# A hybrid decoder trunk on one Trainium2 core: square roots of the mixer's norms by Newton steps instead of ScalarE's Sqrt

## The chip, the core and the metric

The kernel runs on one core of a Trainium2 chip. The core's engines take instructions from queues of their own: TensorE (PE, matrix products; its weight loads are shown apart as PEld), VectorE (DVE), ScalarE (ACT, activation functions and copies), GpSimd (POOL) and SyncE (SP, which issues most DMAs). They wait for one another by semaphores. The metric is the time of one execution on the device in microseconds (us), lower is better. ACT computes functions by tables; where the next function is not in the table that is loaded, an instruction ACT_TABLE_LOAD stands ahead of it, with the line of the function that needs it.

## What is computed

A trunk of two layers on x of 512 tokens by 1024 (one sequence), in float32. Layer 0 mixes tokens by a gated DeltaNet, layer 1 by sliding-window attention on a shared key and value; each layer ends with a convolutional gated MLP. The part that the change touches is the mixer:

```python
q = l2norm(q) * 128 ** -0.5          # l2norm: x * rsqrt(sum(x * x) + 1e-6)
k = l2norm(k)                        # 8 key heads, each serving 2 of 16 value heads
...
o = chunked_gated_delta_rule(q, k, v, g, beta)
...
o = rmsnorm(o, out_norm_w) * silu(z) # rmsnorm: mean over the 128 of a head
return o @ w_out
```

## The kernel before, in words

Every product with a weight matrix is made of three passes: the weights and the moving tile are each split into a rounded part and a rest (whi/wlo and xh/xl, or yh/yl), and whi·xh, whi·xl and wlo·xh are added (L162 to L164). ACT casts the rounded part (L132 for weights, L168 for rows), DVE subtracts for the rest (L133, L169). A pass moves 512 columns. Tokens stand in 4 chunks of 128 (NC = 4).

The mixer treats its heads in four groups g = 0 to 3, each of 2 key heads and 4 value heads. For a group the jobs are: key projections K (convolution and silu at L277 to L281), key norms B, the decay matrices and key products P (exponentials at L475), a triangular solve I (DVE, L555 to L561, levels L at L587 to L615), queries Q, query norms R, A, key tokens T, values V (turned on PE at L198, then scaled by ACT at L538), the scan C0 to C3 over the four chunks, and output norms N; then z (gate projection, silu L705) and g (gate: the output is loaded from DRAM, scaled by ACT at L720, turned on PE at L198, multiplied on DVE at L723).

A table of words (ORDER, five lines) and a table of shifts (SHIFT) give each job a priority. A scheduler makes the order of each engine's instructions from these priorities and from its own reckoning of how long each takes; so an instruction that is added or taken out can move others on all engines.

**Key norms** (key_norms, L426 to L456): PE multiplies the keys with themselves (L433), DVE takes the diagonal and sums it (L437, L443) into sse, adds EPS (L444) and takes the reciprocal rk2 (L445) for brk and kap (L449, L455). ACT takes the square root nk (L446), which only the scaling of the turned values reads (L538): the values are multiplied by the norm of the key.

**Output norms** (out_norms, L685 to L699): sso holds the sums of squares of the outputs (from ACT, L682). f_c becomes the mean plus a term with EPS (L688, L690), then its square root (ACT, L698) and the reciprocal of it (DVE, L699). f_c is read by the gates (ACT, L720) and by six one-column copies on POOL that hold the later loads of x back (L839).

**Scan** (L622 to L683), one step for each chunk: PE multiplies the state with keys and queries (kS, qS, L635), DVE makes rq (L638), ACT qe (L648), PE pu (L651), ACT copies it to us (L653), PE makes the new state pS and the output po from it (L659), DVE adds (L663, L666, L677, L679), ACT squares for the norm (L682), and SP stores the output to od (L683). Between these stand passes of projections.

**The end of the mixer.** The output projection starts with rows of gated outputs: those of groups 0 to 2 come back from DRAM (yd) and are split (L168, L169) into tiles such as kT, qT, nt, sy, at; the four of group 3 are read from od into dt, scaled, turned and gated without a way through DRAM. Later, rstd_cols takes a square root on ACT (L871) for the norm ahead of the MLP.

Of the kernel before, what the change touches and what calls it, by code (L numbers as in the profile page):

```python
# [8 lines left out]
F32 = mybir.dt.float32  # L9
F32R = mybir.dt.float32r  # L10
BF16 = mybir.dt.bfloat16
AF = mybir.ActivationFunctionType
ALU = mybir.AluOpType
AX = mybir.AxisListType
# [3 lines left out]
P = 128  # L18
T = 512
NC = T // P  # L20
# [21 lines left out]
def kernel(  # L42
# [27 lines left out]
    V, S, G, PE, SP = nc.vector, nc.scalar, nc.gpsimd, nc.tensor, nc.sync  # L70
# [9 lines left out]
    def nm(s):  # L80
        cnt[0] += 1
        return f"{s}_{cnt[0]}"
# [24 lines left out]
    def row(tag, dt=F32, n=T):  # L107
        return main.tile([P, n], dt, tag=tag, bufs=ROWS[tag], name=nm(tag))

    def pair(tag, dt=F32):  # L110
        return main.tile([P, 2, T], dt, tag=tag, bufs=PAIRS[tag], name=nm(tag))

    def bank(tag):
        return psum.tile([P, T], F32, tag=tag, bufs=BANKS[tag], name=nm(tag))

    def const(shape, dt=F32, s="c"):
        return cp.tile(list(shape), dt, name=nm(s))
# [53 lines left out]
    def split_scaled(src, col, hi, lo):  # L171
        S.activation(hi[:], src, AF.Identity, scale=col)  # L172
        V.scalar_tensor_tensor(lo[:], src, col, hi[:].bitcast(F32), op0=ALU.mult, op1=ALU.subtract)
# [8 lines left out]
    def together(makes, *after):  # L182
        first = None
        for make in makes:
            if first is None:
                first = make()
                for a in after:
                    behind(first, a)
            else:
                with tc.high_priority(JUMP):  # L190
                    behind(make(), first)
# [31 lines left out]
    warm = const([P, 1], s="warm")  # L223
    S.activation(warm[:], epsc[:], AF.Sqrt)


    def columns(parts, n, s, q=SP, tag="acc", place="g"):
        st = row(tag, n=P)
        r = 0
        for ap in parts:  # L230
            k = ap.shape[0]
            q.dma_start(st[r : r + k, :], ap)
            r += k
        ps = bank(place)
        PE.transpose(ps[:, :n], st[:n, :], ident[:n, :n])
        t = const([P, n], s=s)
        V.tensor_copy(t[:], ps[:, :n])
        return t
# [16 lines left out]
    for c in range(NC):  # L255
        junk = main.tile([P, D], F32, tag="nt", bufs=2, name=nm("junk"))
        r = const([P, 1], s="rx")
        S.activation(junk[:], xs[c], AF.Square, accum_out=r[:])
        S.activation(r[:], r[:], AF.Sqrt, bias=epsc[:, 0:1], scale=1.0 / D)
        V.reciprocal(r[:], r[:])  # L260
# [14 lines left out]
    def conv_silu(ps, t, o):  # L275
        acc = row("acc")
        S.activation(acc[:], ps[:], AF.Identity, scale=cw_c[:, 96 + t : 97 + t])  # L277
        for d in range(1, 4):
            col = cw_c[:, 32 * (3 - d) + t : 32 * (3 - d) + t + 1]
            V.scalar_tensor_tensor(acc[:, d:], ps[:, : T - d], col, acc[:, d:], op0=ALU.mult, op1=ALU.add)  # L280
        S.activation(o, acc[:], AF.Silu)  # L281
        return o
# [114 lines left out]
    tmp6 = row("p6s")  # L397
    sso = const([P, 16, NC], s="sso")
    f_c = const([P, 16, NC], s="fc")
    sse = const([P, 2, 8, NC], s="sse")  # L400
    nk = const([P, 8, NC], s="nk")
    rk2 = const([P, 8, NC], s="rk2")
# [20 lines left out]
    )  # L423
    fcw = [columns([fconv_rows[l, 0:128, :]], 128, "fcw", tag="f") for l in range(2)]

    def key_norms(g):  # L426
        pr = slice(2 * g, 2 * g + 2)
        st[g]["kk"] = pair("m32")
        for i in range(2):
            kT = st[g]["k"][:, i, :]  # L430
            ps = bank("g")
            cut = [slice(c * P, (c + 1) * P) for c in range(NC)]
            together([lambda cs=cs: PE.matmul(ps[:, cs], kT[:, cs], kT[:, cs], start=True, stop=True) for cs in cut])  # L433
            S.copy(st[g]["kk"][:, i, :], ps[:])
            diag = row("va")
            d3 = diag[:].rearrange("p (c t) -> p c t", c=NC)
            V.tensor_tensor(  # L437
                d3,
                ps[:].rearrange("p (c t) -> p c t", c=NC),
                ident[:].unsqueeze(1).to_broadcast([P, NC, P]),  # L440
                op=ALU.mult,
            )
            V.tensor_reduce(sse[:, 0, 2 * g + i, :], d3, axis=AX.X, op=ALU.add)  # L443
        V.tensor_scalar(sse[:, 0, pr, :], sse[:, 0, pr, :], EPS, None, op0=ALU.add)  # L444
        V.reciprocal(rk2[:, pr, :], sse[:, 0, pr, :])  # L445
        S.activation(nk[:, pr, :], sse[:, 0, pr, :], AF.Sqrt)  # L446
        for i in range(2):
            hs = slice(4 * g + 2 * i, 4 * g + 2 * i + 2)
            V.tensor_tensor(  # L449
                brk[:, hs, :],  # L450
                beta_t[:, hs, :],
                rk2[:, 2 * g + i : 2 * g + i + 1, :].to_broadcast([P, 2, NC]),
                op=ALU.mult,
            )
            V.tensor_tensor(kap[:, hs, :], brk[:, hs, :], egd[:, hs, :], op=ALU.mult)  # L455
# [228 lines left out]

    def out_norms(g):  # L685
        hs = slice(4 * g, 4 * g + 4)
        fs = f_c[:, hs, :].rearrange("p (i j) c -> p i j c", i=2)
        V.tensor_scalar(f_c[:, hs, :], sso[:, hs, :], 1.0 / P, None, op0=ALU.mult)  # L688
        for j in range(2):
            V.scalar_tensor_tensor(  # L690
                fs[:, :, j, :],
                sse[:, 1, 2 * g : 2 * g + 2, :],
                P * EPS,
                fs[:, :, j, :],
                op0=ALU.mult,
                op1=ALU.add,
            )
        S.activation(f_c[:, hs, :], f_c[:, hs, :], AF.Sqrt)  # L698
        V.reciprocal(f_c[:, hs, :], f_c[:, hs, :])  # L699


    def gate_proj(h):
# [32 lines left out]
    def bias_rows():  # L735
# [22 lines left out]
        "L": levels,  # L758
        "C": scan,
        "B": key_norms,  # L760
        "R": query_norms,
        "N": out_norms,
    }
    heads = {"z": 0, "g": 0}
# [679 lines left out]
```

## Time and profile before

| quantity | value |
|---|---|
| time, median of 3 runs | 1415.96 us (1414.63, 1415.96, 1419.01) |
| span of the profiled execution | 1412.6 us; the page gives no other time for it |
| HBM read and written | 133.60 MB and 15.75 MB |
| ACT_TABLE_LOADs in the program | 36 |
| busiest groups | three matmul passes L162, L163, L164: 444.2, 444.0 and 441.9 us shown |

Times in a row of the profile are in us from the start of the span unless marked ns. A group of instructions is told as line, engine, operation, output <- inputs, shape, count, then busy time and mean ns, then the idle time of the engine just ahead of it and what ended it (a bracket in the timeline says the same). Matmuls are pipelined and their ends are modelled: a pass of 512 columns is shown 0.39 long, while the next one starts 0.23 later. So for PE the distance of starts tells more than the duration.

### The profile page before, as it was taken

The numbers are of one execution on the slowest core, as the hardware profiler recorded it, in microseconds if no ns is written. First come the engines' busy times: TensorE is split into PE (matmuls) and PEld (weight loads), VectorE is DVE, ScalarE is ACT, GpSimd is POOL, SyncE is SP. The second block draws the span as 40 slices with busy tenths as digits, with TensorE's granted clock in tenths as the row PEclk, the third lists the DMA queues.
The fourth block names the chain that finished last, engine by engine and source line by source line (L and its number), as shares of the span: only waits on it lengthen the run. The fifth ranks groups of instructions, "written<-read, shape, count | busy, mean of one in ns | idle before, by whom it ended". The sixth has DMA issues, their size and how long they took to land.

```text
span 1412.6 us, 21751 instructions
## 1 busy us (share of the span) xinstructions
PE 1384.7 (98%) x8370; PEld 1167.1 (83%) x8370; DVE 1108.1 (78%) x2070; ACT 748.1 (53%) x1470; POOL 15.6 (1%) x37
## 2 busy tenths in 40 slices
PE   7999999999999999999999999999999999999998
PEld 5787888878877888888988889777788888988897
DVE  4996896978856438879878889788668888878996
ACT  7764566656658225444344446567544444444543
POOL 1000000000100000000000000000000000000000
PEclk9999999999999999999999999999999999999999
DMA  5333254172465323221443223322132231432222
GB/s 161 92 103 115 79 175 126 61 231 84 140 225 159 119 90 112 90 90 46 135 150 119 75 79 109 109 71 76 61 112 90 90 101 49 146 106 82 92 75 75
DMA packets 162299, 151.80 MB, mean 107 GB/s; under 512 B 24148, under 2 KB 150677, under 8 KB 162197
## 3 DMA queue, kind: packets, MB, share of 16 engines
q1 hardware_dynamic: 159938, 150.22, 33.2%
q8 instruction: 66, 1.08, 0.3%
q10 hardware_dynamic: 2259, 0.20, 0.1%
q14 instruction: 36, 0.29, 0.1%
HBM read 133.60 MB, written 15.75 MB: 106 GB/s over the span
## 4 chain that ended last, share of the span: by engine, by line
PE 87%; DVE 6%; DMA 2%; ACT 2%; issue 1%; SPq 0%; DVEq 0%; ACTq 0%
PE d L162 20%; PE d L163 20%; PE d L164 20%; PE g L198 2%; DVE wlo L133 2%; PE d L1054 1%; PE d L1207 1%; PE d L1211 1%; PE d L1209 1%; PE d L1052 1%; PE d L1053 1%; PE s L1054 1%; PE s L1052 1%; PE s L1053 1%; PE s L659 1%
## 5 line engine op out<-in xcount | busy, mean ns | idle before, releaser
L162 PE MATMUL d<-xh,whi 128*128 128x512 f32 x1128 | 444.2, 394 | 0.2
L163 PE MATMUL d<-xl,whi 128*128 128x512 f32 x1128 | 444.0, 394 | 0.0
L164 PE MATMUL d<-xh,wlo 128*128 128x512 f32 x1128 | 441.9, 393 | 0.3 <-DVE wlo L156 0.3
L132 ACT CAST whi<-stage 128x1024 fp32r<-128x1024 f32 (+2 forms) x234 | 227.4, 976 | 247.7 <-PE d L163 165.1
L133 DVE TENSOR_TENSOR wlo<-stage,whi 128x1024 fp32r<-128x1024 f32 (+2 forms) x234 | 263.4, 1128 | 70.4 <-ACT whi L132 69.6
L162 PEld LDWEIGHTS d<-xh,whi 128*128 128x128 f32 x1128 | 211.7, 188 | 44.9 <-ACT xh L172 0.5
L164 PEld LDWEIGHTS d<-xh,wlo 128*128 128x128 f32 x1128 | 211.6, 188 | 44.6 <-DVE wlo L156 0.7
L163 PEld LDWEIGHTS d<-xl,whi 128*128 128x128 f32 x1128 | 211.7, 188 | 43.2 <-issue 0.5
L280 DVE SCALAR_TENSOR_TENSOR acc<-d,cwc,acc 128x511 f32<-128x511 f32 (+2 forms) x96 | 70.7, 739 | 8.7 <-ACT acc L277 7.9
L913 DVE TENSOR_TENSOR sz<-d,p6s 128x512 f32<-128x512 f32 x59 | 40.6, 688 | 42.9 <-PE d L164 40.7
L935 ACT ACTIVATE dt<-dt 128x512 f32<-128x512 f32 x44 | 27.8, 631 | 78.3 <-DVE dt L918 78.3
L918 DVE SCALAR_TENSOR_TENSOR dt<-sz,fcw,dt 128x511 f32<-128x511 f32 (+1 forms) x60 | 44.8, 747 | 1.8 <-ACT dt L916 0.9
L918 DVE SCALAR_TENSOR_TENSOR va<-sz,fcw,va 128x511 f32<-128x511 f32 (+1 forms) x58 | 43.3, 747 | 0.9
L561 DVE TENSOR_TENSOR sT<-sT,p6s 64x31 f32<-64x31 f32 (+15 forms) x124 | 40.9, 330 | 2.0
L555 DVE TENSOR_TENSOR p6s<-sN,sT 64x31 f32<-64x31 f32 (+15 forms) x124 | 40.7, 328 | 1.9
L1276 ACT ACTIVATE dt<-dt,sm 128x256 f32<-128x256 f32 (+1 forms) x64 | 30.1, 471 | 21.5 <-DVE sm L1259 21.5
L132 ACT CAST whi<-st 128x768 fp32r<-128x768 f32 (+1 forms) x30 | 23.7, 792 | 30.5 <-PE g L1053 9.0
L913 DVE TENSOR_TENSOR zl<-d,p6s 128x512 f32<-128x512 f32 x29 | 20.0, 688 | 17.8 <-PE d L164 17.8
L682 ACT ACTIVATE rq<-o 128x128 f32<-128x128 f32 x64 | 19.0, 301 | 25.4 <-DVE o L677 22.3
L937 DVE TENSOR_TENSOR va<-dt,va 128x512 f32<-128x512 f32 x44 | 30.4, 690 | 1.2
L133 DVE TENSOR_TENSOR wlo<-st,whi 128x768 fp32r<-128x768 f32 (+1 forms) x30 | 26.8, 899 | 2.2 <-ACT whi L132 2.2
L916 ACT ACTIVATE dt<-sz,normc,fcw 128x512 f32<-128x512 f32 x30 | 24.5, 815 | 6.5 <-DVE sz L913 6.0
(770 smaller groups left out, 2876.2 us busy)
## 6 DMA issues: line engine op xcount, KB each, us to landing
stage<-in_ffn_w_up_dram SPq DMA_DIRECT2D x44, 1024.0 KB, 4.8
stage<-in_a_w_in_dram SPq DMA_DIRECT2D x23, 1024.0 KB, 5.8
stage<-in_ffn_w_down_dram SPq DMA_DIRECT2D x16, 768.0 KB, 4.3
stage<-in_a_w_out_dram SPq DMA_DIRECT2D x8, 1024.0 KB, 5.0
st<-in_ffn_w_down_dram SPq DMA_DIRECT2D x8, 768.0 KB, 5.3
zd<-sz SPq DMA_DIRECT2D x16, 256.0 KB, 2.6
od<-o SPq DMA_DIRECT2D x16, 256.0 KB
stage<-in_b_w_q_dram SPq DMA_DIRECT2D x4, 1024.0 KB, 5.0
```

What stands on the lines that cost most here:

```text
L132: S.copy(hi[:, :kt, :m], src)
L133: V.tensor_tensor(lo[:, :kt, :m], src, hi[:, :kt, :m].bitcast(F32), op=ALU.subtract)
L162: PE.matmul(ps, hi[:, k, :m], xh[k], start=first and k == 0, stop=False)
L163: PE.matmul(ps, hi[:, k, :m], xl[k][:], start=False, stop=False)
L164: done.append(PE.matmul(ps, lo[:, k, :m], xh[k], start=False, stop=last and k == kt - 1))
L280: V.scalar_tensor_tensor(acc[:, d:], ps[:, : T - d], col, acc[:, d:], op0=ALU.mult, op1=ALU.add)
L555: V.tensor_tensor(tv, N[:, s, s + 1 : 32].unsqueeze(2).to_broadcast([64, n, m]), Tm[:, s : s + 1, 0:m].to_broadcast([64, n, m]), op=ALU.mult,)
L561: V.tensor_tensor(Tm[:, s + 1 : 32, 0:m], Tm[:, s + 1 : 32, 0:m], tv, op=ALU.subtract)
L913: V.tensor_tensor(u[:], ps[:], rs[:], op=ALU.mult)
L918: V.scalar_tensor_tensor(acc[:, d:], u[:, : T - d], tap(2 - d, t), acc[:, d:], op0=ALU.mult, op1=ALU.add)
L937: V.tensor_tensor(b[:], a[:], b[:], op=ALU.mult)
L1276: S.activation(ej, ej, AF.Exp, bias=ngm[:, i : i + 1], scale=-1.0, accum_out=den[:, i : i + 1])
```

## The change

A helper gives the inverse square root: a first guess from the bits of the number read as an integer (one tensor_scalar on DVE), then three Newton steps of four small operations on an engine that is given. For key norms these twelve run on GpSimd, in 128x8 tiles, and a thirteenth multiplies by sse to make the square root from its inverse. For output norms they run on VectorE, in 128x16 tiles, and give f_c at once, so that the reciprocal is not needed; the mean is kept in a new tile fx. The square root at rstd_cols stays as it is.

```diff
+I32 = mybir.dt.int32
...
+    fx = const([P, 16, NC], s="fx")
...
+    def inverse_root(y, x, t, E):
+        V.tensor_scalar(y.bitcast(I32), x.bitcast(I32), -0.5, 1597463007.0, op0=ALU.mult, op1=ALU.add)
+        for _ in range(3):
+            E.tensor_tensor(t, y, y, op=ALU.mult)
+            E.tensor_tensor(t, t, x, op=ALU.mult)
+            E.tensor_scalar(t, t, -0.5, 1.5, op0=ALU.mult, op1=ALU.add)
+            E.tensor_tensor(y, y, t, op=ALU.mult)
+
+    root_t = const([P, 16, NC], s="roott")
...
         V.reciprocal(rk2[:, pr, :], sse[:, 0, pr, :])
-        S.activation(nk[:, pr, :], sse[:, 0, pr, :], AF.Sqrt)
+        inverse_root(nk[:, pr, :], sse[:, 0, pr, :], root_t[:, pr, :], G)
+        G.tensor_tensor(nk[:, pr, :], nk[:, pr, :], sse[:, 0, pr, :], op=ALU.mult)
...
-        fs = f_c[:, hs, :].rearrange("p (i j) c -> p i j c", i=2)
-        V.tensor_scalar(f_c[:, hs, :], sso[:, hs, :], 1.0 / P, None, op0=ALU.mult)
+        fs = fx[:, hs, :].rearrange("p (i j) c -> p i j c", i=2)
+        V.tensor_scalar(fx[:, hs, :], sso[:, hs, :], 1.0 / P, None, op0=ALU.mult)
...
-        S.activation(f_c[:, hs, :], f_c[:, hs, :], AF.Sqrt)
-        V.reciprocal(f_c[:, hs, :], f_c[:, hs, :])
+        inverse_root(f_c[:, hs, :], fx[:, hs, :], root_t[:, hs, :], V)
```

In the changed program lines are numbered one higher up to the helper and 12 or 13 higher behind it, so L538 becomes L551 and L659 becomes L672. PE has the same products in both.

**First place: the first group's key norms on ACT.** Before (nk is the square root, dt an exponential of the decay, va the silu of a value projection; the numbers behind a name only tell tiles apart):

```order
L475 ACTIVATE dt_449<-g_446,ngc_331 128x128 x4
L475 ACTIVATE dt_463<-g_460,ngc_331 128x128 x4
L446 ACT_TABLE_LOAD
L446 ACTIVATE nk_351<-sse_350 128x8
L475 ACT_TABLE_LOAD
L475 ACTIVATE dt_478<-g_475,ngc_331 128x128 x4
L475 ACTIVATE dt_492<-g_489,ngc_331 128x128 x4
L281 ACT_TABLE_LOAD
L281 ACTIVATE va_540<-acc_572 128x512
```

With the change:

```order
L488 ACTIVATE dt_464<-g_461,ngc_331 128x128 x4
L488 ACTIVATE dt_478<-g_475,ngc_331 128x128 x4
L488 ACTIVATE dt_493<-g_490,ngc_331 128x128 x4
L488 ACTIVATE dt_507<-g_504,ngc_331 128x128 x4
L282 ACT_TABLE_LOAD
L282 ACTIVATE va_555<-acc_587 128x512
```

The square root and two table loads are gone ahead of va, and the four exponentials stand together.

**Second place: the last group's scan on PE, from step 0 to step 1.** Rows with line L162 to L164 are passes of a projection, s_ and p_ are banks of the scan. Before, from the last pass ahead of pu (L651) to the passes behind po (L659):

```order
L164 MATMUL d_4404<-xh_196,wlo_4406 128x512
L651 MATMUL s_4176<-rq_4166,sy_3929 128x128 x2
L651 MATMUL s_4176<-rq_4166,sy_4001 128x128 x2
L659 MATMUL p_4184<-us_4181,ktok_3732 128x128 x2
L659 MATMUL s_4183<-us_4181,at_3724 128x128
L659 MATMUL p_4184<-us_4181,ktok_3881 128x128
L659 MATMUL s_4183<-us_4181,at_3724 128x128
L659 MATMUL p_4184<-us_4181,ktok_3881 128x128
L659 MATMUL s_4183<-us_4181,at_3650 128x128 x2
L162 MATMUL d_4625<-kT_4478,whi_4626 128x512
```

With the change (pu is L664, po L672):

```order
L163 MATMUL d_4502<-xh_151,whi_4503 128x512
L164 MATMUL d_4502<-xl_152,whi_4503 128x512
L165 MATMUL d_4502<-xh_151,wlo_4504 128x512
L664 MATMUL s_4263<-rq_4253,sy_4016 128x128 x2
L664 MATMUL s_4263<-rq_4253,sy_4088 128x128 x2
L163 MATMUL d_4502<-xh_160,whi_4503 128x512
L164 MATMUL d_4502<-xl_161,whi_4503 128x512
L165 MATMUL d_4502<-xh_160,wlo_4504 128x512
L163 MATMUL d_4502<-xh_169,whi_4503 128x512
L672 MATMUL p_4271<-us_4268,ktok_3819 128x128 x2
L672 MATMUL s_4270<-us_4268,at_3811 128x128
```

Passes of the last gate projection (d_4502) now stand on both sides of pu, where one pass stood ahead of it and none behind it; the passes of the output projection (d_4625) that filled the scan before stand later.

**Third place: the end of the mixer, on PE and on DVE.** PE ahead of the first turn of dt (L198), before:

```order
L164 MATMUL d_4625<-at_4528,wlo_4655 128x512
L162 MATMUL d_4683<-sy_4498,whi_4684 128x512
L162 MATMUL d_4625<-at_4528,whi_4654 128x512
L163 MATMUL d_4683<-sy_4499,whi_4684 128x512
L164 MATMUL d_4683<-sy_4498,wlo_4685 128x512
L162 MATMUL d_4683<-kT_4508,whi_4684 128x512
L163 MATMUL d_4683<-qT_4509,whi_4684 128x512
L198 MATMUL g_4332<-ident_81,dt_4324 128x128 x4
L163 MATMUL d_4625<-at_4529,whi_4654 128x512
```

With the change (L199):

```order
L163 MATMUL d_4723<-nt_4586,whi_4724 128x512
L163 MATMUL d_4781<-nt_4586,whi_4782 128x512
L164 MATMUL d_4723<-nt_4587,whi_4724 128x512
L165 MATMUL d_4723<-nt_4586,wlo_4725 128x512
L163 MATMUL d_4723<-sy_4596,whi_4724 128x512
L164 MATMUL d_4781<-nt_4587,whi_4782 128x512
L165 MATMUL d_4781<-nt_4586,wlo_4783 128x512
L163 MATMUL d_4781<-sy_4596,whi_4782 128x512
L199 MATMUL g_4430<-ident_81,dt_4422 128x128 x4
L164 MATMUL d_4723<-sy_4597,whi_4724 128x512
```

Before, the output projections have come to the tiles at and kT when the first turn of dt stands in the queue; now they have come to nt and sy. DVE at the output norms, before:

```order
L677 TENSOR_TENSOR o_4278<-rq_4257,s_4273 128x512
L169 TENSOR_TENSOR sy_4519<-zl_4520,sy_4518 128x512
L688 TENSOR_SCALAR fc_349<-sso_348 128x16
L690 SCALAR_TENSOR_TENSOR fc_349<-sse_350,fc_349 128x2x4 x2
L169 TENSOR_TENSOR sy_4519<-sz_4524,sy_4518 128x512
L699 RECIPROCAL fc_349<-fc_349 128x16
L169 TENSOR_TENSOR at_4529<-sz_4530,at_4528 128x512
```

With the change:

```order
L690 TENSOR_TENSOR o_4365<-rq_4344,s_4360 128x512
L170 TENSOR_TENSOR qT_4577<-sz_4582,kT_4576 128x512
L701 TENSOR_SCALAR fx_350<-sso_348 128x16
L703 SCALAR_TENSOR_TENSOR fx_350<-sse_351,fx_350 128x2x4 x2
L429 TENSOR_SCALAR fc_349<-fx_350 128x16
L431 TENSOR_TENSOR roott_382<-fc_349 128x16
L432 TENSOR_TENSOR roott_382<-roott_382,fx_350 128x16
L433 TENSOR_SCALAR roott_382<-roott_382 128x16
L434 TENSOR_TENSOR fc_349<-fc_349,roott_382 128x16
```

Two more rounds of the same four follow at once, so thirteen operations stand one behind the other. Subtractions of the split rows, which stood among the norms (sy, at), come behind them (nt, sy).

## The prediction

> **What bounds the kernel now.** I read the page's busy times first, then its chain of work, then a table of windows, because an average over the whole span says nothing of the stage that changes.
>
> ```profile
> PE 1384.7 (98%) x8370; PEld 1167.1 (83%) x8370; DVE 1108.1 (78%) x2070; ACT 748.1 (53%) x1470; POOL 15.6 (1%) x37
> PE 87%; DVE 6%; DMA 2%; ACT 2%; issue 1%; SPq 0%; DVEq 0%; ACTq 0%
> ```
>
> TensorE (PE) is busy for 98% of the span and carries 87% of the chain; ScalarE (ACT), from which the change takes work, is busy for 53%. The mixer runs from about 40 to 480 us. In a row of the table of windows stand the window, its sum, then PE, PE weight load, DVE, ACT and POOL busy, the granted clock, the DMA share and GB/s:
>
> ```profile
> 40.00:480.00 440.00, 435.05 (x3008) 355.42 (x3007) 341.27 (x719) 271.86 (x688) 9.60 (x20) 1.00 0.43 132
> ```
>
> PE has 440.00 − 435.05 = 4.95 us of idle time in the whole mixer. That is the most that any relief of ACT can win. The list of waits (waiting engine and line, who ended the wait, total, times, longest) says where it lies:
>
> ```profile
> PE g L235 <- DVE onwc L237: 1.7, 1, 1.7
> PE p L659 <- ACT us L653: 1.5, 1, 1.5
> PE g L198 <- ACT ol L720: 1.0, 1, 1.0
> PE d L162 <- ACT kT L168: 0.5, 1, 0.5
> ```
>
> The first is a column load at the start of the mixer that the change doesn't touch. What ACT ends last is 3.0 us, and 2.0 of it (L659, L162) lies in the last group's scan.
>
> **What goes from ACT.** Groups of ACT in 0 to 470 us, with busy time and mean ns of one:
>
> ```profile
> L281 ACT ACT_TABLE_LOAD x8 | 10.3, 1283 | 0.4 <-DVE acc L280 0.3
> L475 ACT ACT_TABLE_LOAD x7 | 9.0, 1283 | 0.1
> L446 ACT ACT_TABLE_LOAD x4 | 5.1, 1283 | 0.1
> L698 ACT ACT_TABLE_LOAD x4 | 5.1, 1283 | 0.1
> L705 ACT ACT_TABLE_LOAD x1 | 1.3, 1283 | 0.0
> L698 ACT ACTIVATE fc<-fc 128x16 f32<-128x16 f32 x4 | 0.9, 216 | 0.0
> L446 ACT ACTIVATE nk<-sse 128x8 f32<-128x8 f32 x4 | 0.8, 209 | 0.0
> ```
>
> By the order of instructions 15 loads go (L446 4, L698 4, L475 4 of 7, L281 2 of 8, L705 1) and one comes back at the first rstd, where no square root has left its table ready. ACT gets 14 × 1.283 + 0.9 + 0.8 = 19.7 us back. None of PE's four waits follows one of these loads directly, so almost all of the 19.7 us lies beside busy PE and is worth nothing by itself. The added load at rstd stands here:
>
> ```profile
> 527.30 0.26 ACT L871 ACTIVATE rt<-g,eps 128x4 f32<-128x4 f32 x1 [2.59 <-PE g L869]
> ```
>
> ACT idles 2.59 us before it, and a load needs no data: the 1.28 us fit into that idle time. I cost it at 0; uncovered it would be 1.3.
>
> **First group's key norms on GpSimd (POOL).** Three views of one place, ACT, DVE and, for a price, the only arithmetic that POOL does on a small tile:
>
> ```profile
> 53.23 1.28 ACT L446 ACT_TABLE_LOAD   x1
> 54.73 1.28 ACT L475 ACT_TABLE_LOAD   x1
> 61.15 1.14 ACT L538 ACTIVATE vt<-g,nk 128x128 f32<-128x128 f32 x4
> 53.69 0.20 DVE L445 RECIPROCAL rk<-sse 128x8 f32<-128x8 f32 x1
> 4.30 0.20 POOL L350 TENSOR_SCALAR_AFFINE_SELECT sk<-sk 128x16 f32<-128x16 f32 x1
> 4.57 0.20 POOL L351 TENSOR_SCALAR_AFFINE_SELECT sk<-sk 128x16 f32<-128x16 f32 x1
> ```
>
> ACT first uses nk at 61.15. Without 1.28 + 0.21 + 1.28 = 2.77 us ahead of it, it asks for nk at about 58.4. POOL begins behind the reciprocal and the bit trick at 53.9, so 13 dependent operations have 4.5 us, 0.35 each. The row's start-to-start distance is 0.27 (4.30 to 4.57): 3.5 us, in time. But that was beside an idle DVE. Beside a busy one POOL's copies of one column look otherwise (first row: ns least/median/most of three copies, and their starts):
>
> ```profile
> L839 POOL COPY st<-fc x3: 389/1199/1962, 359.6 to 361.8; 128x1 f32<-128x1 f32 x3
> 359.14 0.49 POOL L839 COPY f<-fc 128x1 f32<-128x1 f32 x3 [31.57 <-DVE fc L699]
> 360.27 1.21 DVE L133 TENSOR_TENSOR wlo<-stage,whi 128x1024 fp32r<-128x1024 f32 x1
> 361.74 1.21 DVE L133 TENSOR_TENSOR wlo<-stage,whi 128x1024 fp32r<-128x1024 f32 x1
> ```
>
> Three such copies took 0.49 us together beside a DVE operation that reads PSUM; the next one took 1.96 and the last 1.20, each ending 0.05 us behind a DVE subtraction with both inputs in SBUF. So a POOL operation here may cost 0.27 to 1.20 us, the chain 3.5 to 15.6. The Trainium skill ("SBUF — State Buffer", the section on two separate sides) states the reason: GpSimd and VectorE lock a port pair for a whole instruction, a DVE operation with two SBUF inputs among them. The trace agrees with that, copy by copy.
>
> Behind the bit trick the order has four short DVE operations (brk, kap) and eight products over 512 columns, by half of the subtraction's 1.21 about 0.6 each, so about one POOL operation gets through per DVE operation. I take 0.52 each, nearer to the low row than to the high one: 6.7 us, the end at 60.6, ACT waiting 2.2. What does PE lose? Behind vt on ACT stand two casts, a scaling and the silu that makes qT:
>
> ```profile
> L132 ACT CAST whi<-stage 128x1024 fp32r<-128x1024 f32 x3 | 3.2, 1053 | 0.0
> L277 ACT ACTIVATE acc<-d,cwc 128x512 f32<-128x512 f32 x3 | 2.1, 684 | 0.0
> L281 ACT ACTIVATE qT<-acc 128x512 f32<-128x512 f32 x2 | 1.2, 623 | 0.6 <-DVE acc L280 0.6
> ```
>
> That is 1.14 + 2 × 1.05 + 0.68 + 0.62 = 4.5 us from the start of vt until PE's product with qT can begin. By the changed order PE has between the turn of va and that product one more turn (0.9) and 37 passes of 512 columns. The rows of the tail below put passes 0.23 us apart (433.24, 433.47), so 8.4 + 0.9 = 9.3 us. Spare: 9.3 − 4.5, less 0.45 for a hand-over (440.68 to 441.13 below), is 4.3. The wait of 2.2 lies within it: cost **0**. It costs PE time from (4.5 + 4.3)/13 = 0.68 us an operation. In the later groups nk is ready tens of us before the values are turned.
>
> **Output norms on DVE.** Thirteen operations stand for a square root and a reciprocal:
>
> ```profile
> 435.63 0.17 DVE L688 TENSOR_SCALAR fc<-sso 128x16 f32<-128x16 f32 x1 [0.75 <-ACT rq L682]
> 435.83 0.24 DVE L690 SCALAR_TENSOR_TENSOR fc<-sse,fc 128x8 f32<-128x8 f32 x2
> 437.66 0.25 DVE L699 RECIPROCAL fc<-fc 128x16 f32<-128x16 f32 x1 [0.84 <-ACT fc L698]
> ```
>
> One waits for the other, 0.20 us start to start (435.63 to 435.83): 13 × 0.20 = 2.6 us a group in place of 0.25, some 9.4 us of DVE in all; in the mixer's window it has 440.00 − 341.27 = 98.7 us of idle time. For groups 0 to 2 the operations are mixed with others in DVE's order and f_c comes 4 to 5 us later than now; ACT waits longer at L720, while PE runs through projections whose casts are ahead. I cost it at **0**; of PE's wait of 1.0 at L198 (ol) nothing to all may go, so −1 to 0, and I take 0.
>
> **The end of the mixer** decides the sum, since there the last group's norms stand beside the last scan. PE, and the chain of the last output:
>
> ```profile
> 432.09 1.08 PE L659 MATMUL s<-us,at 128*128 128x128 f32 x8
> 433.24 0.39 PE L164 MATMUL d<-sy,wlo 128*128 128x512 f32 x1
> 433.47 0.39 PE L162 MATMUL d<-kT,whi 128*128 128x512 f32 x1
> 441.13 1.20 PE L198 MATMUL g<-ident,dt 128*128 128x128 f32 x4
> 434.25 3.38 DMA od<-o
> 437.65 2.95 DMA dt<-od
> 440.68 0.41 ACT dt L720
> ```
>
> From the last po (432.09) to the first turn of dt PE has 9.04 us to fill, and two DMAs make up 6.3 of them. f_c is not what comes last: now it is done at 437.9, in the changed kernel at 435.6 + 0.45 + 2.6 = 438.7, the data at 440.6. What changes is the filling. Now 34 passes stand there, in the changed order 21, since an output projection that began earlier now begins behind the last gate projection: 13 × 0.23 = 3.0 us less cover. The block of root operations also delays the subtractions nt and sy that some of the 21 passes need, by up to 3 us, but inside the same wait. Now 9.04 less some 0.8 for po (its 1.08 less the overlap of ends) and 34 × 0.23 leaves 0.4 idle; in the changed order 3.4. What comes late on ACT and DVE behind the turns now, some 0.2 to 0.6, can catch up in the longer wait, so of +3.0 I take **+2.4** and keep 3.0 as the other end.
>
> In return the last gate projection fills the scan. Two rows of the scan as it is:
>
> ```profile
> 415.46 0.57 ACT L705 ACTIVATE sz<-d 128x512 f32<-128x512 f32 x1
> 429.13 1.13 DVE L638 SCALAR_TENSOR_TENSOR rq<-s,negegc,vt 128x128 f32<-128x128 f32 x4 [0.35 <-PE s L635]
> ```
>
> Step 0 to 1: in the changed order four passes (0.9) stand between pu and po, where there are none now, and the silu of the gate (0.57) no longer stands ahead of the copy us on ACT; of the 1.5 at L659 about 0.1 is left: **−1.4**. Step 1 to 2: the wait for kT (0.5) goes, its pass stands elsewhere: **−0.5**. Step 2 to 3: the four passes between po and the next kS become none, and a subtraction like the 1.21 above comes between o and rq on DVE, which now idles only 0.35 there: rq starts 0.86 late. I take **+0.8**; 0 to 1.2 is possible.
>
> Sum: −1.4 − 0.5 + 0.8 + 2.4 = **+1.3 us**. The profiled execution has a span of 1412.6, and the page gives no time around it; the median of the three runs, 1415.96, is 3.4 above it. I add the difference to both: span 1413.9, time **1417.3**.
>
> **The rivals.** *ACT's freed time shows on PE.* For it: ACT ends 3.0 us of PE's waits. Against it: none stands behind a load. At best the waits at L659, L162 and L198 go and the tail fills itself: −3.0 to −4.95, 1411 to 1413. Chance 0.09; over 0.3% (4.2 us) it is nearly the whole idle time of the mixer, so it is mostly within the bound.
>
> *GpSimd's chain is late* (slower). The thirteen operations at L446's place cost more than 0.68 each, as the copies at 359.6 did, or the first starts late. At 1.20 they end at 69.5, ACT is 11.1 late, PE loses 11.1 − 4.3 = 6.8: 1424.1. For it: the copies. Against it: DVE's operations at that place are shorter than 1.21. Chance 0.15. The Trainium skill ("GPSIMD Engine Reference", Instruction dispatch) says the first call of a freshly loaded kernel pays about 6 us that no row shows; by it, an estimate, the chain ends at 66.6 and the time is near 1421. The trace speaks neither way: POOL's first select starts without a gap, and none of its arithmetic appears.
>
> *The tail costs in full* and the scan wins nothing: 3.0 of lost cover, 1.2 in step 2 to 3 and a late split or two, +4 to +5: 1420 to 1421. Chance 0.10.
>
> That the loads don't go is excluded by the order. The forecast, between 1413 and 1420, keeps 0.66.
>
> **How the numbers follow.** About 0.3% is what a measurement of this kernel can tell from no change: 1411.7 to 1420.2. Faster: the end of the first rival, 0.07. Slower: the second rival, half of the third and an edge of the forecast, 0.23. Same: 0.70. The range reaches from 1412.5, most of what the waits can give back, to 1422, with a POOL operation of about 0.9 us.
>
> **What would show it.** PE idle in 40 to 480 us stays near 6; 14 loads fewer; a wait of 3 us for dt at the first turn; no wait of 1.45 in the last group's first step; nk ready before about 62.7. A PE wait for qT near 70 us, or POOL's thirteen taking over 8.8 us, would make the prediction wrong; so would a load at rstd with PE waiting for it.

## The result and the profile after

The changed kernel takes 1426.76 us (median of 6 runs, 1423.57 to 1428.54), beside 1417.78 for the kernel before (6 runs, 1414.63 to 1419.52): ratio 1.0066, 95% interval 1.0052 to 1.0080. It is slower, by 9.0 us, where 1417.3 was forecast and 1422 was the end of the range. The profiled execution took 1426.47 with a span of 1424.7; its span is 12.1 us longer than that of before.

The changed kernel's page, busy times and chain by engine:

```profile
PE 1389.8 (98%) x8370; PEld 1170.4 (82%) x8370; DVE 1112.9 (78%) x2122; ACT 728.4 (51%) x1448; POOL 34.1 (2%) x89
PE 86%; DVE 7%; ACT 3%; DMA 3%; issue 1%; POOL 0%; SPq 0%; DVEq 0%; ACTq 0%
```

ACT has 19.7 us less work, the very sum of the prediction, and the kernel is slower all the same. PE's busy time has grown by 5.1 us with the same 8370 products, so some of them ran slower. The mixer's row in the table of windows (columns as before) has the rest:

```profile
40.00:480.00 440.00, 428.15 (x2953) 347.81 (x2952) 341.20 (x765) 246.79 (x659) 29.11 (x74) 0.99 0.43 131
```

PE idles 440.00 − 428.15 = 11.85 us in place of 4.95, 6.9 more, and the granted clock is 0.99 in place of 1.00. 5.1 and 6.9 make the 12.1 but for 0.1. The list of PE's waits says what it idles for:

```profile
PE d L163 <- ACT nt L169: 3.9, 1, 3.9
PE g L199 <- ACT va L282: 2.7, 2, 1.7
PE d L163 <- DVE acc L281: 0.9, 1, 0.9
PE g L199 <- ACT h L858: 0.8, 1, 0.8
```

None of these stood among the waits of before. If the starts of PE's products in both traces are set against one another at equal numbers of columns moved, the changed kernel is 0.6 us late when before stands at 260 us, 7.5 at 280, 5.6 at 300 and again at 390 (between these the comparison swings by up to 2 us, where the two orders differ), 6.0 at 420, 7.1 at 430, 13.7 at 440 and about 12 from 460 to the end. So the loss has two places: the values of the second group (g = 1) near 270 us, about 6, and the end of the mixer, 5.4 counted from 430 us and 6.5 counted from 420.

**First place.** The timeline of PE, and of DVE and ACT ahead of it (start, duration, engine, line, what, and in brackets the idle time before it with its releaser):

```profile
263.99 0.15 DVE L431 TENSOR_TENSOR roott<-fc 128x16 f32<-128x16 f32 x1
264.07 0.40 DVE L574 TENSOR_TENSOR sT<-sT,p6s 64x247 f32<-64x247 f32 x1
271.91 0.50 PE L163 MATMUL d<-xh,whi 128*128 128x512 f32 x1 [0.94 <-DVE acc L281]
272.91 0.64 ACT L282 ACTIVATE va<-acc 128x512 f32<-128x512 f32 x1
273.61 0.66 PE L199 MATMUL g<-ident,va 128*128 128x128 f32 x4 [0.96 <-ACT va L282]
276.01 1.12 PE L199 MATMUL g<-ident,va 128*128 128x128 f32 x4 [1.75 <-ACT va L282]
277.35 0.63 PE L163 MATMUL d<-xh,whi 128*128 128x512 f32 x1
277.78 0.63 PE L164 MATMUL d<-xl,whi 128*128 128x512 f32 x1
```

PE takes its turns of va as they stand in its queue, and the last two of the three come before ACT has made va; ACT waits for the convolution sums acc, which DVE, busy without a gap from 260 to 276, delivers late. A root operation itself takes little there: the next DVE operation starts 0.08 us behind it. The thirteen of this group start between 263.3 and 270.1, so by an estimate from that row they make the sums some 1.0 us later. Windows of the same stretch (window, length, PE busy, granted clock, DMA share, GB/s):

```profile
270.00:274.00 4.00, 2.10 (x13) 1.00 0.00 0
274.00:276.00 2.00, 0.26 (x3) 0.76 0.00 0
276.00:282.00 6.00, 5.99 (x17) 0.51 0.56 177
282.00:284.00 2.00, 2.00 (x10) 1.00 0.01 1
```

PE waits 0.94, 0.96 and 1.75 us, and from within the last wait it runs at half clock up to 282, passes 0.43 us apart (277.35 to 277.78) where they were 0.23. These 3.65 us of waits thus cost about 7 (0.6 to 7.5 above), of which 1.9 come back by 300; before, PE stood 1.0 us for ol in that stretch.

**Second place.** The queue of SP and what waits for it. First before, then after:

```profile
425.02 1.69 SPq L824 DMA_DIRECT2D sz<-yd  x2
433.66 0.38 SPq L824 DMA_DIRECT2D sz<-yd  x1
434.25 0.32 SPq L683 DMA_DIRECT2D od<-o  x1
```

```profile
428.54 0.32 SPq L718 DMA_DIRECT2D zd<-sz  x1
431.93 0.43 SPq L836 DMA_DIRECT2D sz<-yd  x1
432.41 0.43 SPq L123 DMA_DIRECT2D stage<-in_a_w_out_dram  x1
435.63 0.32 SPq L696 DMA_DIRECT2D od<-o  x1
436.00 0.99 SPq L836 DMA_DIRECT2D sz<-yd  x2
442.20 0.62 ACT L169 CAST nt<-sz 128x512 fp32r<-128x512 f32 x1 [5.27 <-DMA sz<-yd]
442.87 1.22 PE L163 MATMUL d<-nt,whi 128*128 128x512 f32 x2 [3.94 <-ACT nt L169]
```

Before, the rows of yd are loaded into sz one after another, and all of them are issued ahead of the last store of od. Now the last gate projection, moved into the scan, still holds a tile sz until its store at 428.54; a row goes into it at 431.93, and the next two loads into sz stand in SP's queue behind the last store of od and are issued at 436.00. PE stands 3.94 us for the cast of the first of them, and half clock follows (443 to 446 us: 0.55 granted).

The loads are not only late, they are also slow. These rows of the list of transfers in 428 to 440 us (before, then after) end with the median us from issue to landing:

```profile
sz<-yd SPq DMA_DIRECT2D x3, 256.0 KB, 3.5
```

```profile
sz<-yd SPq DMA_DIRECT2D x3, 256.0 KB, 6.3
```

In the changed kernel 1024 KB of weights (stage) are issued at 432.41, just ahead of them; before, the same load stood at 416.60. By these numbers up to 2.8 of the 3.94 us may be due to that. Two of the kernels below that lose at the end in the same way have the weights at 426.21 (key_only) and 431.13 (before_z2) and loads of 5.6 and 6.1 us; no run changes the place of the weights alone.

**What went as forecast.** The end of the first group's norm on GpSimd, and the load that came back at rstd:

```profile
54.04 0.20 POOL L431 TENSOR_TENSOR roott<-nk 128x8 f32<-128x8 f32 x1 [34.14 <-DVE nk L429]
54.32 0.20 POOL L432 TENSOR_TENSOR roott<-roott,sse 128x8 f32<-128x8 f32 x1
60.23 0.20 POOL L459 TENSOR_TENSOR nk<-nk,sse 128x8 f32<-128x8 f32 x1
60.47 1.14 ACT L551 ACTIVATE vt<-g,nk 128x128 f32<-128x128 f32 x4 [2.12 <-POOL nk L459]
537.28 1.28 ACT L883 ACT_TABLE_LOAD   x1
539.85 0.26 ACT L883 ACTIVATE rt<-g,eps 128x4 f32<-128x4 f32 x1 [1.29 <-PE g L881]
```

### The profile page after: what moved, and what is told of

Its sections match the earlier page's. It is cut to its first block, busy times and chain, and to the rows that moved or that the text cites. A ratio compares the mean times of both kernels' runs of the same rounds, so it can differ in the third digit from the quotient of the medians.

```text
span 1424.7 us, 21839 instructions
## 1 busy us (share of the span) xinstructions
PE 1389.8 (98%) x8370; PEld 1170.4 (82%) x8370; DVE 1112.9 (78%) x2122; ACT 728.4 (51%) x1448; POOL 34.1 (2%) x89
## 4 chain that ended last, share of the span: by engine, by line
PE 86%; DVE 7%; ACT 3%; DMA 3%; issue 1%; POOL 0%; SPq 0%; DVEq 0%; ACTq 0%
PE d L163 19%; PE d L164 19%; PE d L165 19%; PE g L199 2%; DVE wlo L134 2%; PE d L1066 1%; PE d L1064 1%; PE d L1065 1%; PE d L1219 1%; PE d L1223 1%; PE d L1221 1%; PE s L1066 1%; PE s L664 1%; PE s L1064 1%; PE s L1065 1%
## 5 line engine op out<-in xcount | busy, mean ns | idle before, releaser
L164 PE MATMUL d<-xl,whi 128*128 128x512 f32 x1128 | 445.5, 396 | 0.0
L164 PEld LDWEIGHTS d<-xl,whi 128*128 128x128 f32 x1128 | 212.3, 188 | 43.4 <-issue 0.5
```

What stands on the lines that cost most here:

```text
L164: PE.matmul(ps, hi[:, k, :m], xl[k][:], start=False, stop=False)
```

## The experiments

Two theories stood against each other. ORDER: the new instructions cost nothing; the scheduler, given other instructions, put PE's projections, the value turns and the row loads in another order, and that costs the time. COST: the Newton operations on DVE and GpSimd themselves make others late. ORDER can be tried in both directions, since a number in SHIFT (a job's place, higher is later) changes the order and no instruction.

Half of the change each. key_only, against the changed kernel; out_only takes back the other half:

```diff
-        inverse_root(f_c[:, hs, :], fx[:, hs, :], root_t[:, hs, :], V)
+        S.activation(f_c[:, hs, :], fx[:, hs, :], AF.Sqrt)
+        V.reciprocal(f_c[:, hs, :], f_c[:, hs, :])
```

```diff
-        inverse_root(nk[:, pr, :], sse[:, 0, pr, :], root_t[:, pr, :], G)
-        G.tensor_tensor(nk[:, pr, :], nk[:, pr, :], sse[:, 0, pr, :], op=ALU.mult)
+        S.activation(nk[:, pr, :], sse[:, 0, pr, :], AF.Sqrt)
```

> Key norms by Newton steps on GpSimd, output norms by ScalarE's square root as before. Theory ORDER (the loss comes from where the scheduler puts value turns and row loads, in two places): by the order of instructions the second group (g = 1) stands as before (51, 59 and 81 passes from the last scan product to its first three value turns; before 52, 59, 82; changed kernel 43, 47, 47), the end of the mixer as in the changed kernel (21 passes to the first dt turn, 4 row loads ahead of the last store of od; before 34 and 11). So no loss at 270 us, the whole one at the end: +5 to +7 us over before. Theory COST (the 13 operations a group on VectorE are the loss): they are gone here, so within 1 us of before.

> Output norms by Newton steps on VectorE, key norms by ScalarE's square root as before. ORDER: the second group's value turns stand after 20, 40 and 40 passes, more crowded than in the changed kernel, the end of the mixer has 44 passes and 11 loads as or better than before: a loss of 5 to 9 us near 270 us and none at the end, so +4 to +9 us. COST: VectorE's operations are all there, so the same +12 us as the changed kernel, at both places.

The kernel before with another order and no Newton step at all (before_r4: query norms two places earlier; before_z2: gate projections two later):

```diff
-SHIFT = {"R": 6, "B": -28, "g": -40, "K": -1, "N": 7, "C": -2, "P": -3}
+SHIFT = {"R": 4, "B": -28, "g": -40, "K": -1, "N": 7, "C": -2, "P": -3}
...
+SHIFT = {"R": 6, "B": -28, "g": -40, "K": -1, "N": 7, "C": -2, "P": -3, "z": 2}
```

> The kernel before with one number of the table of shifts changed (R 6 to 4): no Newton step at all. The second group's value turns now stand after 46, 48 and 48 passes, the end of the mixer has 44 passes and 11 loads. ORDER: PE waits for value turns near 270 us as in the changed kernel, +4 to +7 us. COST: nothing was added, 0 within 1.5 us.

> The kernel before with one number of the table of shifts added (z: 2): no Newton step. The second group stands as before (52, 60, 82 passes), the end of the mixer as in the changed kernel (21 passes, 4 loads ahead of the last store). ORDER: a wait of about 4 us for a cast of nt behind a row load near 440 us, +5 to +7 us. COST: 0 within 1.5 us.

The table has all runs. "Turns" are the passes that PE has between the last po of group 1 and its three value turns, by the order; "loads" is the number of row loads, of 12, that stand ahead of the last store of od in SP's queue. The last columns are PE's busy time (of 40.00) and granted clock in two windows of the profiled execution. Each ratio goes by the runs of before that lay beside it (medians 1415.98 to 1417.78).

| kernel | time, us | ratio [95%] | turns | loads | 260:300 | 420:460 |
|---|---|---|---|---|---|---|
| before | 1415.98 (29 runs) | 1 | 52, 59, 82 | 11 | 38.82, 1.00 | 39.39, 1.00 |
| after | 1426.76 | 1.0066 [1.0052, 1.0080] | 43, 47, 47 | 4 | 36.35, 0.91 | 34.21, 0.96 |
| key_only | 1420.88 | 1.0035 [1.0023, 1.0047] | 51, 59, 81 | 4 | 40.00, 1.00 | 34.29, 0.96 |
| out_only | 1426.93 | 1.0075 [1.0063, 1.0088] | 20, 40, 40 | 11 | 37.00, 0.96 | 38.82, 0.92 |
| before_r4 | 1431.79 | 1.0105 [1.0089, 1.0120] | 46, 48, 48 | 11 | 35.94, 1.00 | 37.03, 0.90 |
| before_z2 | 1425.22 | 1.0060 [1.0047, 1.0072] | 52, 60, 82 | 4 | 40.00, 1.00 | 33.87, 0.96 |
| key_a2 | 1416.36 | 1.0000 [0.9988, 1.0011] | 51, 59, 81 | 11 | 38.88, 1.00 | 37.74, 0.96 |
| after_2steps | 1423.33 | 1.0055 [1.0034, 1.0075] | 47, 53, 53 | 4 | 36.98, 0.91 | 35.30, 0.96 |
| after_4steps | 1426.32 | 1.0068 [1.0054, 1.0082] | 48, 53, 53 | 5 | 36.14, 0.91 | 35.49, 0.96 |
| after_loads | 1432.84 | 1.0116 [1.0099, 1.0133] | – | – | 36.33, 0.91 | 33.64, 0.87 |
| after_rows | 1428.73 | 1.0081 [1.0062, 1.0100] | 43, 47, 47 | 7 | 36.32, 0.96 | 35.97, 0.91 |
| after_z2_rows | 1424.60 | 1.0055 [1.0037, 1.0072] | 48, 59, 76 | 12 | 39.55, 1.00 | 39.53, 1.00 |
| after_both | 1422.20 | 1.0030 [1.0018, 1.0043] | 92, 96, 107 | 12 | 39.58, 1.00 | 38.77, 1.00 |
| before_rows | 1421.60 | 1.0027 [1.0016, 1.0038] | 52, 59, 82 | 11 | 39.20, 1.00 | 37.72, 0.96 |
| after_gr | 1419.66 | 1.0020 [1.0009, 1.0031] | 43, 47, 47 | 11 | 36.34, 0.91 | 39.49, 1.00 |
| after_gr_c0 | 1429.08 | 1.0088 [1.0069, 1.0107] | 46, 58, 76 | 12 | 38.05, 1.00 | 38.05, 0.85 |
| after_gr_v3 | 1416.95 | 1.0003 [0.9992, 1.0014] | 65, 71, 82 | 11 | 40.00, 1.00 | 39.37, 1.00 |
| before_gr | 1414.55 | 0.9988 [0.9975, 1.0000] | 52, 59, 82 | 12 | 39.56, 1.00 | 37.94, 0.96 |

key_only has before's turns and no loss near 270, and after's loads and the loss at the end: ORDER, though its 4.8 us are just under the 5 to 7 expected. out_only loses near 270 as expected, but 10.9 us in all, nearer to the 12 of COST than to the 4 to 9 of ORDER: some 6 us go in the last scan (410 to 440 us), where neither theory had put a loss. before_r4 shows the same two losses without one Newton operation. It loses 4.6 us near 270, in the same manner; its wait in 260 to 300 us:

```profile
PE g L198 <- ACT va L281: 3.0, 2, 1.8
```

It loses 15 in all, not 4 to 7: the last scan again. before_z2 shows the second place without a Newton operation, at 9.2 us in all where 5 to 7 were expected (its trace is 3.9 late at 390 us already):

```profile
441.39 1.22 PE L162 MATMUL d<-nt,whi 128*128 128x512 f32 x2 [3.77 <-ACT nt L168]
```

Next, key_a2 keeps key_only's Newton steps and puts the job A two places later ("A": 2 added to SHIFT), which by the order brings the loads back ahead of the store:

> As key_only (Newton steps on GpSimd for the key norms alone), with one number added to the table of shifts (A: 2) so that both places stand as before: value turns of the second group after 51, 59 and 81 passes, 34 passes to the first dt turn, 11 row loads ahead of the last store of od. ORDER: the +5 us of key_only go away, within 1.5 us of the kernel before. Rival OPERATIONS (the Newton steps on GpSimd and the missing table loads shift things at a cost of their own): +3 us or more is left.

It came out at ratio 1.0000: key_only's loss was its order, and GpSimd's Newton steps cost nothing that can be measured (the interval reaches from 1.7 us faster to 1.6 slower).

More or less root work at the same places (`range(3)` in the helper becomes `range(2)` or `range(4)`; two steps are less exact):

> The changed kernel with two Newton steps in place of three (a less exact root): 8 operations fewer on VectorE than with four in each group, 4 fewer than in the changed kernel. Up to 400 us its order on PE is that of the kernel with four steps (value turns of the second group after 47, 53, 53 passes). ORDER: the loss near 270 us is there, 3 to 7 us, and differs from that with four steps by less than 1 us. COST: it is smaller than with four steps by 8 x 0.2 us a group or more.

> The changed kernel with four Newton steps: value turns of the second group after 48, 53, 53 passes, 26 passes and 5 row loads at the end of the mixer. ORDER: at 400 us within 1 us of the kernel with two steps. COST: at 400 us 2 to 5 us later than the kernel with two steps (8 operations more in each of three groups, each 0.2 us or more on the path).

At equal numbers of columns moved, 2 and 4 steps lose 6.4 and 6.8 us near 270, so eight more DVE operations change that loss by only 0.4. But ORDER's forecast for 400 us missed: there the kernel with four steps is 4.8 us behind the one with two, as COST had said (2 to 5), and its median is 3.0 later. From 40 to 400 us PE idles 4.8 us with two steps and 7.9 with four; 0.95 of the difference lies in the first group, 0.5 from 200 to 240, 0.8 near 270 and 0.9 from 300 to 320. So root operations do cost time once there are enough of them. The first group shows how. ACT and PE with four steps:

```profile
61.49 1.15 ACT L551 ACTIVATE vt<-g,nk 128x128 f32<-128x128 f32 x4 [3.04 <-POOL nk L459]
```

```profile
PE g L521 <- ACT qT L282: 1.0, 1, 1.0
```

ACT waits 3.04 us for nk where it waited 2.12, and PE waits 1.0 for qT, which it did not with three steps. The chain ends 1.0 us later, at 61.46, so its cover ends at about 60.5 us.

What holds the row loads? after_loads issues them from GpSimd's queue instead of SP's:

```diff
-                SP.dma_start(yr[:], yd[2 * h2 + j])
+                G.dma_start(yr[:], yd[2 * h2 + j])
```

> The changed kernel with the twelve row loads for the output projection issued by GpSimd's queue instead of SyncE's, so that none stands behind the last store of od. All up to the last scan step keeps its order; 30 passes instead of 21 then stand ahead of the first dt turn. Theory LOAD (the load of nt, held behind that store, sets the end of the mixer): the wait of 3.9 us for nt goes and the time falls by 4 to 6 us. Rival DMA CHAIN (store of od, then load of dt, each twice as long as before beside other transfers, would end at the same 445 us anyhow): the wait moves from nt to dt, and the time falls by 0 to 2.5 us.

Both theories missed: the kernel got 6 us slower than the changed one, and the wait only changed its name:

```profile
439.49 0.62 ACT L169 CAST kT<-sz 128x512 fp32r<-128x512 f32 x1 [5.39 <-DMA sz<-yd]
```

Its chain of waits (start, us, engine, what) goes from this load back to the gate's store out of the same tile:

```profile
430.33 2.35 DMA zd<-sz
433.22 6.25 DMA sz<-yd
```

So not the queue alone but the tile sets the load's start (theory SLOT). Rows may be given another tile in the list that they rotate through; acc was tried first, in four kernels (after_both has "R": 8 and "V": -2 as well, after_z2_rows "z": 2; before_rows is the control):

```diff
-        "u": ["sz", "sz", "zl"],
+        "u": ["acc", "sz", "zl"],
```

> The changed kernel, only that the rows loaded for the output projection go into the tiles acc, sz, zl in turn instead of sz, sz, zl. By the order the second group stands as in the changed kernel (43, 47, 47 passes), and 21 passes stand ahead of the first dt turn as there, but 7 row loads instead of 4 stand ahead of the last store of od, among them that of nt. Theory SLOT (the two tiles sz are still held by the last gate projection and by rows in work, so the load of nt is late): the wait of 3.9 us for nt goes, the time falls by 2 to 5 us against the changed kernel, so +6 to +9 us over before. Rival COVER (21 passes don't last until dt is there, whatever nt does): PE waits for dt instead, the time falls by less than 1.5 us.

> The changed kernel with all its Newton steps, the rows as in after_rows, and two numbers of the table of shifts other (R 8, V -2). Value turns of the second group after 92, 96 and 107 passes (before 52, 59, 82), of the third after 98, 104 and 113; 46 passes to the first dt turn and 12 row loads ahead of the last store. ORDER: no wait for value turns near 270 us and none for nt: within 2.5 us of the kernel before. COST: the operations are all there, +8 us or more is left.

> The kernel before with the rows in acc, sz, zl (no Newton step): second group as before (52, 59, 82), 31 passes and 11 loads at the end. A control: no one of the theories gives it more than 1.5 us either way.

All four missed: against the runs of before beside them after_rows lost 11.35 us (6 to 9 expected; the wait for nt became one of 4.0 for sy), after_both 4.8 (at most 2.5), after_z2_rows 7.2 (−2 to +4) and the control 4.2 (at most 1.5). The tile acc is also used in the attention. By 500 us after_both is only 2.3 us late and after_rows 3.4 earlier than after, but then both lose some 5.4 from 920 to 1000 us, and the control and after_z2_rows lose some 4 there. With the tile gr:

```diff
-        "u": ["sz", "sz", "zl"],
+        "u": ["gr", "sz", "zl"],
```

> The changed kernel with the rows for the output projection in the tiles gr, sz, zl in turn. The second group stands as in the changed kernel (43, 47, 47 passes); at the end 37 passes and 11 row loads stand ahead of the dt turn and of the last store (changed kernel 21 and 4). SLOT: the loss near 270 us stays (+6 us), the one at the end goes to 0 to 2 us: +6 to +8.5 us over before. Rival OPERATIONS (the end loses by the root operations themselves): +11 us as the changed kernel.

> The kernel before with the rows in gr, sz, zl: the second group as before; 43 passes and 12 loads at the end. A control without a Newton step: within 2.5 us of before by every theory.

The loss at the end goes, the one near 270 stays, and the kernel before gains next to nothing from the same tile. In all after_gr is 3.7 us over before, less than the 6 to 8.5 expected: its trace is 4.6 late at 390 us and only 1.8 at 430, so some of the first loss is made up in the last scan. In these windows of after_gr (columns as above) both can be read:

```profile
260.00:300.00 40.00, 36.34 (x164) 0.91 0.35 108
420.00:460.00 40.00, 39.49 (x221) 1.00 0.63 198
```

Last, the value job three places earlier ("V": -3), with all Newton steps in place, and a rival order in which the scan is not drawn forward ("C": 0):

> As after_gr, with V: -3 in the table of shifts: value turns of the second group after 65, 71 and 82 passes, 39 passes and 11 loads at the end. All Newton steps are there. ORDER: within 3 us of before. COST: +6 us or more, the loss near 270 us is left.

> As after_gr, with C: 0 in the table of shifts: value turns of the second group after 46, 58 and 76 passes, 43 passes and 12 loads at the end. ORDER: 0 to +4 us (the end, with the output projection begun late in the last scan, as in out_only, may cost a few). COST: +6 us or more with a wait for value turns near 270 us.

```profile
260.00:300.00 40.00, 40.00 (x208) 1.00 0.35 102
420.00:460.00 40.00, 39.37 (x219) 1.00 0.59 190
```

These are after_gr_v3's windows: both losses gone, 1416.95, ratio 1.0003. That is not quite nothing: beside before_gr, which has the same tile, it is 2.4 us slower, and ahead of the first place, from 160 to 240 us, its PE idles 2.95 us (for ol, va and other results of ACT and DVE) where before's does not idle at all:

```profile
160.00:240.00 80.00, 77.05 (x573) 1.00 0.43 131
```

Whether that is this order or the root operations, no run tells. after_gr_c0 repaired the first place too, but came out 13.1 us over before, where 0 to 4 were expected: its order cost some 12 us from 390 to 420 (PE waited 2.4 us at once for ol, and the clock is 0.74 from 400 to 440). No version beats before by what can be measured.

## Why the prediction was wrong

**Right.** The bound was PE, and ACT's 19.7 us, beside busy PE, were worth nothing; the 14 loads went and the one at rstd fitted into ACT's idle time. GpSimd's chain ended at 60.43 us (60.23 + 0.20), against 60.6 forecast from 0.52 an operation, ACT waited 2.12 against 2.2, and PE lost nothing. The rows show why a price between the ends fitted: 0.28 start to start (54.04 to 54.32) beside a DVE operation that reads PSUM, about 0.6 beside DVE's products with both inputs in SBUF. The first operation started 0.08 us behind the end of the bit trick on DVE (53.96). So the 6 us that the Trainium skill states ("GPSIMD Engine Reference", Instruction dispatch) for the first call of a freshly loaded kernel are not seen here.

**Failed: "For groups 0 to 2 … PE runs through projections whose casts are ahead. I cost it at 0".** The wait for ol that this is about did stay small, 0.6 us after 1.0. What failed is what it takes for granted, that PE runs through its work in the old order. I had read the order at three places, all where instructions were replaced or near the end; in group 1 it moved the value turns from 52, 59 and 82 passes behind the scan to 43, 47 and 47. Their convolution sums are not ready so early, PE stands, and the step costs about 6 us, not 0. That the order is the main cause is shown from both sides: before_r4 has the loss without root operations, after_gr_v3 has them without the loss. The root operations have a small share that no run separates: some 1.0 us by the estimate above, and PE idles 3.0, 3.65 and 3.9 us from 260 to 280 with two, three and four steps.

**Failed in size: the end of the mixer, "+2.4", 3.0 at the other end.** It cost 5.4 to 6.5. The mechanism that I priced, 13 passes less of cover, is there, but I followed PE and took it that the rows of yd would be loaded as before. The forecast wait of 3 us for dt did not come, since PE stood for nt first. The tile sz that the moved gate projection holds longer decides when nt is loaded: in after_gr another tile takes the loss away, while another queue alone does not (after_loads). How much of it is the slower transfer beside the weights is not shown. And I priced waits by their length alone: behind 3.94 us of wait PE ran at 0.55 of its clock for 3 us.

**Mis-sized, without effect.** The spare cover of GpSimd's chain: 4.3 us over a wait of 2.2 was forecast, so an end at 62.7 was to be harmless; after_4steps shows that about 60.5 is the limit. Between the scaling and the silu for qT I had left out DVE's additions to acc, for which that silu waits. With three steps the chain ended just in time, so this was luck. The output norms were to take some 9.4 us more of DVE; its busy time grew by 4.8 in all (1108.1 to 1112.9), since a root operation between others takes 0.08 and not 0.20. The scan's gain was near right: PE idled 1.97 us from 410 to 430 before and 0.35 now, as these rows of the windows (the columns of all engines) show, 1.6 against 1.9 forecast. First before, then after:

```profile
410.00:420.00 10.00, 8.55 (x59) 7.67 (x58) 6.89 (x14) 5.74 (x18) 0.00 (x0) 1.00 0.59 197
420.00:430.00 10.00, 9.48 (x54) 8.13 (x53) 6.71 (x19) 7.00 (x27) 0.00 (x0) 1.00 0.72 250
```

```profile
410.00:420.00 10.00, 10.00 (x73) 8.33 (x73) 5.13 (x10) 5.50 (x18) 0.00 (x0) 1.00 0.41 141
420.00:430.00 10.00, 9.65 (x64) 8.54 (x63) 5.02 (x15) 6.09 (x18) 0.00 (x0) 1.00 0.40 130
```

The 3.4 us between span and time were no property of the program: each execution of after lies 1.8 above its span (1426.47 and 1424.7). The execution of before that was profiled was a quick one (1414.63, its clock at 1.00 all through the mixer), which is why the traces differ by 12.1 and the medians by 9 to 11. In before_gr and key_a2, whose medians are no later than before's, the profiled execution has 0.96 from 420 to 460 us, so up to 2 us of what the second place shows can be chance of the execution.

The rivals had GpSimd's chain, ACT and the tail; none had another group's order. The slower side of the forecast came out, by a cause that it didn't name.

**Left open.** Orders with 44 passes ahead of the first turn of dt (out_only, before_r4) lose 6 to 8 us in the last scan, and after_gr_c0, with 43, loses 12; before_gr, with 43, does not. Much of it is the clock: from 418 to 426 us it is at 0.50 in all three and at 1.00 before, behind waits of PE for steps of the triangular solve (0.5 to 0.8 us each in out_only). Why these orders leave the solve uncovered was not followed up. Why rows in acc cost the attention 4 to 6 us was not followed up either.

## What to carry to other kernels

Work taken from an engine that isn't the bound is worth nothing by itself, but where a scheduler sets the order, taking it away can reorder every engine, and here that alone ranged from nothing to 15 us. So compare the whole order and not only the places that were edited: count the passes between a producer and the next instruction that needs it on the in-order engine, follow each tile of a rotating list, with the DMA that frees it, to its next use, and look for a large load that now stands beside a small one that is waited for. And try the change, and the old kernel too, with another priority or two before its cost is put down to the operations: one number took 4.5 us off key_only, one number and a tile's name 9.8 off the changed kernel.

## What was not expected of the hardware

Short waits can cost more than their length. In the first place no wait is longer than 1.75 us, but PE is busy for only 2.10 + 0.26 = 2.36 of the 6 us up to 276, and the clock is then granted at 0.51 for 6 us. They do not always do so. In before_r4 the same place has waits of 1.30 and 1.75 us, and the clock stays:

```profile
272.00:278.00 6.00, 2.95 (x19) 1.00 0.02 3
278.00:284.00 6.00, 5.62 (x25) 1.00 0.57 175
```

That it has a little more work in it need not be the reason. Near 44 us every kernel has one wait of 1.6 to 1.9 us for onwc, which none of the changes is about. In the trace of the changed kernel the clock stays behind it; in that of before_z2, where the wait is as long, it falls to half (first after, then before_z2):

```profile
45.66 0.48 PE L236 MATMUL g<-ident,f 128*128 128x128 f32 x2 [1.70 <-DVE onwc L238]
46.00:49.00 3.00, 3.00 (x23) 1.00 0.95 282
```

```profile
44.64 0.53 PE L235 MATMUL g<-ident,f 128*128 128x128 f32 x2 [1.70 <-DVE onwc L237]
45.00:48.00 3.00, 3.00 (x12) 0.50 0.94 281
```

The clock falls there in 9 of the 18 traces. In the clock records of the traces it stays down for 3.41 us at this place and for 6.83 near 270 us in the changed kernel, which by half clock costs some 1.7 and 3.4 us, an estimate. So the length of a wait does not decide alone whether it costs more than itself, and one trace of a kernel can differ from the next by such a step.

The Trainium skill ("TensorE: Matmul & The Clock Gate", the section on HAM oscillation) gives the rule to allow no PE idle gap over some 3.4 us. These rows show that gaps of half that length can suffice, which goes better with what Part 1 of that page of the Trainium skill says, that activity is watched in a free-running window of that length.

GpSimd's small operations more than doubled in distance, from 0.28 to about 0.6 us, while DVE ran operations with both inputs in SBUF, and went back to 0.28 (59.95 to 60.23) when DVE's next product read PSUM: the price of this chain on GpSimd depends on what DVE runs beside it.
